# The hand-over between stages of an encoder trunk, put into program order on TensorE, VectorE and ScalarE

## The chip, the cores and the metric

The kernel runs on one core of a Trainium2 chip. A core has TensorE (PE, the matrix products), VectorE (DVE) and GpSimd (POOL) for element-wise work, ScalarE (ACT) for activations and copies, and SyncE (SP), which only starts transfers. Each engine works through its own queue of instructions in order, and waits there on semaphores that other engines raise. The metric is the device time of one execution in microseconds (us).

## The reference

Two layers over 512 tokens of width 1024, in fp32. Each layer is a feed-forward half-step, a mixer with three attentions, and a second feed-forward half-step, each between two RMS norms:

```python
y = swiglu(rmsnorm(h, ffn1_pre_g[l]), ffn1_w_gu[l], ffn1_w_down[l])
h = h + 0.5 * rmsnorm(y, ffn1_post_g[l])
u = rmsnorm(h, mix_pre_g[l]); proj = u @ w_in[l]
...
h = h + rmsnorm(merged @ w_out[l], mix_post_g[l])
y = swiglu(rmsnorm(h, ffn2_pre_g[l]), ffn2_w_gu[l], ffn2_w_down[l])
h = h + 0.5 * rmsnorm(y, ffn2_post_g[l])
```

So a stage ends with a product y, the mean square of y over the width, the new h, and from it the operand of the next stage's first product.

## The kernel before

**Data.** Activations lie transposed: h is eight tiles of 128 features x 512 tokens, and so are y and the operand X. Every fp32 product is made of three matmuls (mm3, L245): high part by high part, high by low, low by high. The high parts are made on ScalarE and the low parts on VectorE: for weights at L201 and L202 (tile w, from the loaded tile wr), for X at L316 and L317 (`operand`: X high = h times the gain, X low = the rest). HALVES are the two halves of 256 tokens.

**The end of a stage** (`end`, L361). All column blocks but the last are made over all 512 tokens. The last block (a feed-forward stage) or the last two (a mixer) are made in two halves by `part` (L390): `part(0)`, then `part(1)`; in a feed-forward stage a half has 22 steps of three matmuls, in a mixer 2 x 8 steps. Each block's y is copied on ScalarE, and its squares are added up in the tile ss (L311). After a part come the *sums*: matmuls of ss with ones (L291), 128x1 each, then a scale by VectorE (L293), a square root on ScalarE (L294) and a reciprocal on VectorE (L295); and the *spread*: matmuls that repeat the resulting scales over 128 partitions (L282), into a PSUM tile at. Then `refresh(i)` (L410) makes the half i of the new h and X: y times the scales for eight tiles on VectorE (L413), h plus y (L416; on VectorE for tiles 2 and 5, on GpSimd for the other six), X high on ScalarE and X low on VectorE.

**The begin of the next stage** (`begin`, L321). The first three column blocks are made in two halves as well, with the weights kept: `dense` over the eight X for the first half (3 blocks x 3 matmuls for each X), `refresh(1)`, then the second half. After that the squares of the new h are added up (L310, L311), and sums and spread over all 512 tokens (`finish_rms`, L338) give rB, by which the stage's products are multiplied. In a feed-forward stage that happens in the middle of the product u1 (L478), in a mixer after the product `second`.

There are five such hand-overs: from a feed-forward stage to a mixer at 344 and 1598 us, from one feed-forward stage to the next at 1238 us, and from a mixer to a feed-forward stage at 884 and 2132 us.

**What sets the order.** The program is written for a tile framework whose scheduler sorts the instructions of every engine by its own model of readiness; the order written in the code is only its input. Inside `tc.manual_schedule(engines=...)` the named engines keep the order of the code instead. The kernel before uses that at none of the places above. Weights are loaded by ScalarE's queue (L188) in tiles of 512 KB, each of which `ensure` (called by `wblk`) turns into two pairs of high and low halves ahead of their use; there are four buffers for these pairs, and some more that are lent for the hand-over.

Of the kernel before, what the change touches and what calls it, by code (L numbers as in the profile page):

```python
# [16 lines left out]
P = 128  # L17
# [94 lines left out]
def encoder_kernel(ctx: ExitStack, tc: tile.TileContext, order, xT, wts, cols, rows, rpb, consts, tables, out):  # L112
# [134 lines left out]
        PE.matmul(acc, w[0], x[1], start=False, stop=False)  # L247
        PE.matmul(acc, w[1], x[0], start=False, stop=stop)  # L248

    def dense(blocks, X, tags=("mm",), cs=WHOLE, accs=None, ws=None, midway=None):  # L250
        accs = accs or [bank(tags[i % len(tags)]) for i in range(len(blocks))]
        n = len(X)
        kept = []
        for k in range(n):
            if midway and k == n // 2:
                midway()
# [7 lines left out]
    def dense1(name, l, c, X, r0=0, tag="mm", midway=None):  # L264
        return dense([(name, l, r0, c)], X, (tag,), midway=midway)[0]

    def split(src, tag="a", scale=None, shape=(P, T)):
        hi = big(tag, F32R, shape, name="hi")
# [16 lines left out]
        return rep[:, : nt * P]  # L285


    def inv_rms(squares, n, nt):
        tot = bank("o")
        for t in range(nt):  # L290
            PE.matmul(tot[:, t : t + 1], squares[:, t * P : (t + 1) * P], ones[:, 0:1], start=True, stop=True)  # L291
# [4 lines left out]
        return spread(r, nt)  # L296

    class Squares:
        def __init__(self):
# [38 lines left out]
    def finish_rms(s, rB):  # L338
        rep = inv_rms(s.acc, D, NT)
        V.tensor_copy(rB, rep)  # L340
        return rep

    def pair(name, dt=F32R):
# [17 lines left out]
    def end(name, l, X, group, tail, gcol, after, hold=()):  # L361

        ys = singles("y")
        y = [ys(b) for b in range(KD)]
        s = Squares()

        def take(b, acc, cs):
            s.add(V if b == KD - 1 else G, acc[:, cs], cs)
            A.activation(y[b][:, cs], acc[:, cs], AF.Copy, scale=gcol(b))

        if hold:
            at = len(order) + (KD - tail) * len(X)
# [11 lines left out]
        def scales(i):  # L384
            hs = HALVES[i]
            return inv_rms(s.acc[:, hs], D, 2)

        held = {}

        def part(i):  # L390
            for m in range(KD - tail, KD):
                acc, cs = bank("mm" if m % 2 else "at"), HALVES[i]
                ks = list(range(len(X)))
                if i and not hold:
                    ks.reverse()
                for n, k in enumerate(ks):
                    if (m, k) not in held:
# [10 lines left out]
        reps, Xn = [], fresh() if after else None  # L408

        def refresh(i):  # L410
            hs = HALVES[i]
            for b in range(KD):
                V.tensor_tensor(out=y[b][:, hs], in0=y[b][:, hs], in1=reps[i], op=ALU.mult)  # L413
            for b in range(KD):
                adder = V if b % 3 == 2 else G
                adder.tensor_tensor(out=h[b][:, hs], in0=h[b][:, hs], in1=y[b][:, hs], op=ALU.add)  # L416
                if after:
                    operand(Xn, i, b, after)
                else:
                    nc.sync.dma_start(out[b * P : (b + 1) * P, hs], h[b][:, hs])  # L420
# [34 lines left out]
    def ffn(l, which, refresh, X):  # L455
# [164 lines left out]
        finish(0, g0, u0)  # L620
        finish(1, g1, u1)
        for m in range(2, PLAIN):
            finish(m, dense1(gu, l, m, X), dense1(gu, l, KF + m, X, tag="at"))
        while later:
            later.pop(0)()
        divide("22")
# [279 lines left out]
    def mixer(l, refresh, X):  # L906
        w = "w_in"
        firsts = [(w, l, 0, QA), (w, l, 0, KA), (w, l, 0, VA)]
        first, s = begin(refresh, X, firsts, [holder("tx")] * 2)
        second = [dense1(w, l, c + 1, X) for c in (QA, KA)[:SECOND]]  # L910
        rB = big("rr", name="rB")
        rep = finish_rms(s, rB)
# [207 lines left out]

    X = fresh()

    def refresh(i):
        for b in range(KD):
            operand(X, i, b, pre(0, 0))

    refresh(0)
    for l in range(L):
        with open_phase("f"):
            refresh, X = ffn(l, 1, refresh, X)  # L1130
# [4 lines left out]
    refresh(1)  # L1135
    assert len(order) == NBLOCKS, (len(order), NBLOCKS)


# [54 lines left out]
```

## Time and profile before

| | |
|---|---|
| median of 3 runs | 2518.18 us (2516.23 to 2518.66) |
| the profiled execution | 2517.49 us, span 2515.7 us |
| mean granted TensorE clock | 0.994 |
| TensorE busy | 2471.4 us (98%) |
| VectorE busy | 1702.3 us (68%) |
| ScalarE busy | 1260.5 us (50%) |
| GpSimd busy | 197.6 us (8%) |

The profile is of one execution. Busy time of an engine is the sum of its instructions' spans; since matmuls are pipelined, one that starts 0.12 us after the one before is shown with a span of 0.28 us, and the pace of TensorE is read from starts. The views used below: the page (a summary), the waits (idle time of an engine put down to the instruction that released it), the windows (busy time and instruction count of each engine in a stretch of time, with the granted clock, 1.00 being full speed), and the timeline (single instructions of an engine with start, duration, line, tiles and, in brackets, the idle time ahead and its releaser; equal neighbours are put together as "x8").

### The profile page before, as it was taken

Reading aid. Unit: us, or ns where it says so; the run is one execution under the profiler, and the core shown is the slowest. Engines: PE = TensorE matmul, PEld = TensorE weight load, DVE = VectorE, ACT = ScalarE, POOL = GpSimd, SP = SyncE. Lnnn points to the kernel's source line nnn. Section 1 sums busy time; section 2 is a strip of 40 time slices with the busy share of each in tenths; the row PEclk is TensorE's granted clock in tenths of the full one; section 3 lists DMA queues with packets and bytes.
Section 4 is the critical chain, followed back from the end, with each engine's and each line's share of the span. In section 5 each row is a group of like instructions: output and inputs, shape, how many; then the busy total and the mean of one; then the engine's idle time right before and its main releaser. Section 6 shows DMA issues by size and latency. Waiting matters only on the chain.

```text
span 2515.7 us, 38188 instructions
## 1 busy us (share of the span) xinstructions
PE 2471.4 (98%) x14586; PEld 2181.1 (87%) x14586; DVE 1702.3 (68%) x3062; ACT 1260.5 (50%) x2447; POOL 197.6 (8%) x177
## 2 busy tenths in 40 slices
PE   9999999999999999999999999999999999999998
PEld 8999888888778889998889998888787788899987
DVE  8877248857767478773388772588676764887723
ACT  6555245645555455553355553546455554555532
POOL 0000020000111120000100000200011112100002
PEclk9999999999999999999999999999999999999999
DMA  4333337434443323333233333374344423233232
GB/s 153 109 106 97 100 101 208 115 109 127 117 126 98 108 65 116 101 101 93 92 93 109 110 93 93 125 197 116 107 126 133 119 90 110 65 116 103 91 103 84
DMA packets 97398, 278.21 MB, mean 111 GB/s; under 512 B 13504, under 2 KB 17984, under 8 KB 97216
## 3 DMA queue, kind: packets, MB, share of 16 engines
q10 hardware_dynamic: 41184, 149.52, 19.5%
q1 hardware_dynamic: 56032, 126.27, 17.7%
q8 instruction: 114, 1.87, 0.3%
q14 instruction: 68, 0.56, 0.1%
HBM read 231.16 MB, written 6.29 MB: 94 GB/s over the span
## 4 chain that ended last, share of the span: by engine, by line
PE 85%; DVE 7%; DMA 4%; issue 1%; SPq 1%; ACT 1%; POOL 1%; POOLq 0%; DVEq 0%; ACTq 0%
PE mm L650 19%; PE mm L248 14%; PE mm L247 14%; PE mm L246 14%; PE at L246 4%; PE at L247 4%; PE at L248 4%; PE at L650 3%; DMA wr<-in_wts_dram 1%; DVE X L317 1%; DMA sh<-raw 1%; PE at L884 1%; DVE y L413 1%; PE at L856 1%; PE o L888 1%
## 5 line engine op out<-in xcount | busy, mean ns | idle before, releaser
L202 DVE TENSOR_TENSOR w<-wr,w 128x512 fp32r<-128x512 f32 x568 | 406.6, 721 | 408.7 <-ACT w L201 406.6
L201 ACT ACTIVATE w<-wr 128x512 fp32r<-128x512 f32 x568 | 354.3, 629 | 554.1 <-PE at L248 269.3
L248 PE MATMUL mm<-X,w 128*128 128x512 f32 (+1 forms) x1096 | 418.5, 383 | 7.2 <-DVE w L202 7.2
L247 PE MATMUL mm<-X,w 128*128 128x512 f32 (+1 forms) x1096 | 419.0, 383 | 4.2 <-DVE X L317 4.2
L246 PE MATMUL mm<-X,w 128*128 128x512 f32 (+1 forms) x1096 | 419.3, 384 | 2.9 <-ACT w L201 1.8
L650 PE MATMUL mm<-lt,h 128*128 128x256 f32 x1024 | 289.8, 283 | 0.0
L650 PE MATMUL mm<-ht,h 128*128 128x256 f32 x1024 | 289.8, 283 | 0.0
L650 PE MATMUL mm<-ht,l 128*128 128x256 f32 x1024 | 289.8, 283 | 0.0
L248 PEld LDWEIGHTS mm<-X,w 128*128 128x128 f32 x1096 | 209.8, 192 | 41.5 <-DVE w L202 8.4
L247 PEld LDWEIGHTS mm<-X,w 128*128 128x128 f32 x1096 | 210.1, 192 | 39.2 <-DVE X L317 6.4
L246 PEld LDWEIGHTS mm<-X,w 128*128 128x128 f32 x1096 | 210.0, 192 | 36.2 <-ACT w L201 2.0
L650 PEld LDWEIGHTS mm<-lt,h 128*128 128x128 f32 x1024 | 196.0, 191 | 0.0
L650 PEld LDWEIGHTS mm<-ht,l 128*128 128x128 f32 x1024 | 196.0, 191 | 0.0
L650 PEld LDWEIGHTS mm<-ht,h 128*128 128x128 f32 x1024 | 196.0, 191 | 0.0
L543 DVE TENSOR_TENSOR r<-wr,wr 128x1024 f32<-128x1024 f32 x64 | 78.5, 1226 | 117.9 <-DMA wr<-in_wts_dram 115.1
L311 POOL TENSOR_TENSOR ss<-ss,sq 128x512 f32<-128x512 f32 (+1 forms) x38 | 47.3, 1245 | 1357.6 <-ACT sq L310 1356.5
L247 PE MATMUL mm<-a,w 128*128 128x512 f32 (+1 forms) x432 | 152.7, 354 | 0.0
L650 PE MATMUL mm<-h,h 128*128 128x256 f32 x512 | 145.7, 285 | 3.4 <-DVE v L704 3.3
L650 PE MATMUL mm<-h,l 128*128 128x256 f32 x512 | 144.9, 283 | 0.0
L650 PE MATMUL mm<-l,h 128*128 128x256 f32 x512 | 144.9, 283 | 0.0
L271 ACT ACTIVATE hi<-at 128x256 fp32r<-128x256 f32 (+2 forms) x168 | 76.5, 473 | 73.1 <-PE at L884 29.4
L247 PE MATMUL mm<-lo,w 128*128 128x512 f32 (+1 forms) x288 | 110.6, 384 | 0.0
(270 smaller groups left out, 5814.7 us busy)
## 6 DMA issues: line engine op xcount, KB each, us to landing
wr<-in_wts_dram ACTq DMA_DIRECT2D x285, 512.0 KB, 3.5
wr<-in_wts_dram SPq DMA_DIRECT2D x130, 512.0 KB, 3.5
st<-hi SPq DMA_DIRECT2D x84, 128.0 KB, 2.4
st<-lo SPq DMA_DIRECT2D x84, 128.0 KB, 3.3
sh<-raw SPq DMA_DIRECT2D x104, 64.0 KB, 3.4
sw<-lo SPq DMA_DIRECT2D x36, 128.0 KB, 3.8
sw<-hi SPq DMA_DIRECT2D x36, 128.0 KB, 2.7
braw<-in_rpb_dram SPq DMA_DIRECT2D x16, 256.0 KB
```

Source lines behind the costliest of these rows:

```text
L201: A.activation(hi, raw, AF.Copy)
L202: V.tensor_tensor(out=lo, in0=raw, in1=f(hi), op=ALU.subtract)
L246: PE.matmul(acc, w[0], x[0], start=start, stop=False)
L247: PE.matmul(acc, w[0], x[1], start=False, stop=False)
L248: PE.matmul(acc, w[1], x[0], start=False, stop=stop)
L271: A.activation(hi, src, AF.Copy)
L311: eng.tensor_tensor(out=self.acc[:, cs], in0=self.acc[:, cs], in1=sq[:, cs], op=ALU.add)
L317: V.scalar_tensor_tensor(out=lo[:, hs], in0=h[b][:, hs], scalar=gcol(b), in1=f(hi)[:, hs], op0=ALU.mult, op1=ALU.subtract)
L413: V.tensor_tensor(out=y[b][:, hs], in0=y[b][:, hs], in1=reps[i], op=ALU.mult)
L543: V.tensor_tensor(out=W[g]["r13"], in0=base, in1=raws[g][0], op=ALU.add)
L650: PE.matmul(acc, ws[i], xs[j], start=start and k == n == 0, stop=stop and k == HK - 1 and n == 2, skip_group_check=True,)
L856: PE.matmul(sp, qs, sk[0][:, j0 * P : j1 * P], start=True, stop=False)
```

## The change

Nothing is computed that was not computed before, with the same instructions on the same engines; what changes is where they stand.

- `inv_rms` is taken apart into `sums` and `spread`, so that the two can be put at different places. `dense` takes a table of hooks: a function to be called ahead of step k.
- TensorE keeps the program's order (`fix`) from `part(0)` on until behind the next stage's `finish_rms` (`loose`).
- In that order the sums of the first half stand ahead of step 4 of `part(1)` (behind 12 matmuls), the spread and `refresh(0)` ahead of step 10 (behind 30). In the next stage's first half, eight steps of nine matmuls, the second half's sums stand ahead of step 2, spread and `refresh(1)` ahead of step 5. The sums for rB stand ahead of step 5 (feed-forward) or 4 (mixer) of the following product, their spread three steps into the third product (feed-forward) or behind the product (mixer).
- In `refresh`, VectorE and ScalarE keep the program's order: first all y and h (y0, h0, y1, h1 and so on, h on the engine it had), then all eight X.

```diff
-        def refresh(i):
-            hs = HALVES[i]
-            for b in range(KD):
-                V.tensor_tensor(out=y[b][:, hs], in0=y[b][:, hs], in1=reps[i], op=ALU.mult)
-            for b in range(KD):
-                adder = V if b % 3 == 2 else G
-                adder.tensor_tensor(out=h[b][:, hs], in0=h[b][:, hs], in1=y[b][:, hs], op=ALU.add)
-                if after:
-                    operand(Xn, i, b, after)
...
+        def refresh(i):
+            hs = HALVES[i]
+            rep = spread(rs[i], 2)
+            with tc.manual_schedule(engines={V.engine, A.engine}):
+                for b in range(KD):
+                    V.tensor_tensor(out=y[b][:, hs], in0=y[b][:, hs], in1=rep, op=ALU.mult)
+                    adder = V if b % 3 == 2 else G
+                    adder.tensor_tensor(out=h[b][:, hs], in0=h[b][:, hs], in1=y[b][:, hs], op=ALU.add)
+                for b in range(KD):
+                    if after:
+                        operand(Xn, i, b, after)
...
-        part(0)
-        reps.append(scales(0))
-        ensure(stream["made"] + (0 if hold else 2))
-        refresh(0)
-        part(1)
-        reps.append(scales(1))
-        return refresh, Xn
+        fix()
+        part(0)
+
+        def first_half():
+            ensure(stream["made"] + (0 if hold else 2))
+            refresh(0)
+
+        part(1, {4: lambda: total(0), 10: first_half})
+        return {2: lambda: total(1), 5: lambda: refresh(1)}, Xn
...
-        accs, ws = dense(first, X, ("mm", "at"), HALVES[0])
-        refresh(1)
+        accs, ws = dense(first, X, ("mm", "at"), HALVES[0], hooks=refresh)
         dense(first, X, (), HALVES[1], accs, ws)
...
-        u1 = dense1(gu, l, KF + 1, X, tag="at", midway=lambda: finish_rms(s, rB))
+        r = []
+        u1 = dense1(gu, l, KF + 1, X, tag="at", hooks={5: lambda: r.append(sums(s.acc, D, NT))})
+        third = dense1(gu, l, 2, X, hooks={3: lambda: finish_rms(r[0], rB)})
+        loose()
```

What this does to the order, at the places that the prediction speaks of:

**VectorE, first hand-over, second half.** The tiles of y are 2756 to 2759 (two tiles in each, hence x2), those of h and X are numbered from h_74 and X_3438 on; L413, L416 and L317 are y, h and X low. Before:

```order
L413 TENSOR_TENSOR y_2756<-y_2756,at_3674 128x256 x2
L413 TENSOR_TENSOR y_2757<-y_2757,at_3674 128x256 x2
L413 TENSOR_TENSOR y_2758<-y_2758,at_3674 128x256 x2
L413 TENSOR_TENSOR y_2759<-y_2759,at_3674 128x256 x2
L317 SCALAR_TENSOR_TENSOR X_3438<-h_74,colt,X_3438 128x256
L317 SCALAR_TENSOR_TENSOR X_3439<-h_75,colt,X_3439 128x256
L416 TENSOR_TENSOR h_76<-h_76,y_2757 128x256
L317 SCALAR_TENSOR_TENSOR X_3441<-h_77,colt,X_3441 128x256
L317 SCALAR_TENSOR_TENSOR X_3442<-h_78,colt,X_3442 128x256
L416 TENSOR_TENSOR h_79<-h_79,y_2758 128x256
```

The same place after (L428 and L430 are y and h there; the L311 between them are the squares of h's first half):

```order
L428 TENSOR_TENSOR y_2756<-y_2756,at_3742 128x256 x2
L428 TENSOR_TENSOR y_2757<-y_2757,at_3742 128x256
L311 TENSOR_TENSOR ss_3879<-ss_3879,sq_3893 128x256
L430 TENSOR_TENSOR h_76<-h_76,y_2757 128x256
L428 TENSOR_TENSOR y_2757<-y_2757,at_3742 128x256
L428 TENSOR_TENSOR y_2758<-y_2758,at_3742 128x256 x2
L311 TENSOR_TENSOR ss_3879<-ss_3879,sq_3896 128x256
L430 TENSOR_TENSOR h_79<-h_79,y_2758 128x256
L428 TENSOR_TENSOR y_2759<-y_2759,at_3742 128x256 x2
L317 SCALAR_TENSOR_TENSOR X_3438<-h_74,colt,X_3438 128x256
L317 SCALAR_TENSOR_TENSOR X_3439<-h_75,colt,X_3439 128x256
```

X_3438, the first X that TensorE needs, stood behind the eight y, and now stands behind the eight y, two h and two additions of squares.

**VectorE, first hand-over, first half**, after the change (L202 makes low parts of weights):

```order
L428 TENSOR_TENSOR y_2757<-y_2757,at_3585 128x256
L428 TENSOR_TENSOR y_2758<-y_2758,at_3585 128x256
L202 TENSOR_TENSOR w_3579<-wr_3577,w_3579 128x512
L202 TENSOR_TENSOR w_3582<-wr_3577,w_3582 128x512
L428 TENSOR_TENSOR y_2758<-y_2758,at_3585 128x256
L430 TENSOR_TENSOR h_79<-h_79,y_2758 128x256
L428 TENSOR_TENSOR y_2759<-y_2759,at_3585 128x256 x2
L317 SCALAR_TENSOR_TENSOR X_3438<-h_74,colt,X_3438 128x256
...
L317 SCALAR_TENSOR_TENSOR X_3445<-h_81,colt,X_3445 128x256
L202 TENSOR_TENSOR w_3628<-wr_3626,w_3628 128x512
L202 TENSOR_TENSOR w_3643<-wr_3626,w_3643 128x512
L311 TENSOR_TENSOR ss_2963<-ss_2963,sq_3667 128x256
```

Two low parts of weights stand among the y, and the addition to ss_2963, which the second half's sums read, stands behind all eight X and two more weights. Before, it stood behind the eight X and three weights, with one weight among the y, one behind the h, and X_3438 and X_3439 ahead of the h.

**TensorE, first hand-over, next stage's first half.** mm and at_3677 are the accumulators of the three blocks, o the sums, at_3742 and at_3674 the spread's result. Before, around the spread:

```order
L246 MATMUL mm_3682<-X_3444,w_3711 128x256
L247 MATMUL mm_3682<-X_3444,w_3711 128x256
L248 MATMUL mm_3682<-X_3444,w_3712 128x256
L246 MATMUL mm_3684<-X_3444,w_3727 128x256
L282 MATMUL at_3674<-cons,rs_3670 128x128 x2
L246 MATMUL at_3683<-X_3438,w_3591 128x256
L247 MATMUL at_3683<-X_3438,w_3591 128x256
```

After:

```order
L248 MATMUL mm_3678<-X_3439,w_3582 128x256
L291 MATMUL o_3697<-ones,ss_2963 128x1 x2
L246 MATMUL mm_3676<-X_3440,w_3582 128x256
...
L248 MATMUL mm_3678<-X_3442,w_3643 128x256
L282 MATMUL at_3742<-cons,rs_3701 128x128 x2
L246 MATMUL mm_3676<-X_3443,w_3643 128x256
```

Before, two of the three blocks ran over the X first, the sums stood at the fifth X, and behind the spread the whole third block (24 matmuls) was left beside the rest of the two. After, all three blocks take each X together, the sums stand behind two X (18 matmuls), and behind the spread three X (27 matmuls) are left.

More of the change, by code (lines that the diff above doesn't have):

```diff
@@ L254, in dense @@
         for k in range(n):
-            if midway and k == n // 2:
-                midway()
+            if k in hooks:
+                hooks[k]()
             x = X[k][0][:, cs], X[k][1][:, cs]
@@ L285, in spread, with sums @@
         return rep[:, : nt * P]
-    def inv_rms(squares, n, nt):
+    def sums(squares, n, nt):
         tot = bank("o")
@@ L295, in inv_rms @@
         V.reciprocal(out=r[:, :nt], in_=r[:, :nt])
-        return spread(r, nt)
+        return r
     class Squares:
@@ L336, in begin, with finish_rms, fix, loose @@
         return accs, s
-    def finish_rms(s, rB):
-        rep = inv_rms(s.acc, D, NT)
+    def finish_rms(r, rB):
+        rep = spread(r, NT)
         V.tensor_copy(rB, rep)
         return rep
+    fixed = []
+    def fix():
+        fixed.append(tc.manual_schedule(engines={PE.engine}))
+        fixed[-1].__enter__()
+    def loose():
+        if fixed:
+            fixed.pop().__exit__(None, None, None)
     def pair(name, dt=F32R):
@@ L382, in end, with part @@
                 take(m + b, acc, WHOLE)
-        def scales(i):
-            hs = HALVES[i]
-            return inv_rms(s.acc[:, hs], D, 2)
         held = {}
-        def part(i):
+        def part(i, hooks={}):
+            step = 0
             for m in range(KD - tail, KD):
@@ L396, in part @@
                 for n, k in enumerate(ks):
+                    if step in hooks:
+                        hooks[step]()
+                    step += 1
                     if (m, k) not in held:
@@ L407, in end, with total @@
         A.activation(dummy, y[KD - tail - 1][:, 0:1], AF.Sqrt, scale=0.0)
-        reps, Xn = [], fresh() if after else None
+        rs, Xn = [], fresh() if after else None
+        def total(i):
+            rs.append(sums(s.acc[:, HALVES[i]], D, 2))
         def refresh(i):
             hs = HALVES[i]
-            for b in range(KD):
-                V.tensor_tensor(out=y[b][:, hs], in0=y[b][:, hs], in1=reps[i], op=ALU.mult)
-            for b in range(KD):
-                adder = V if b % 3 == 2 else G
-                adder.tensor_tensor(out=h[b][:, hs], in0=h[b][:, hs], in1=y[b][:, hs], op=ALU.add)
-                if after:
-                    operand(Xn, i, b, after)
-                else:
-                    nc.sync.dma_start(out[b * P : (b + 1) * P, hs], h[b][:, hs])
-        part(0)
-        reps.append(scales(0))
-        ensure(stream["made"] + (0 if hold else 2))
-        refresh(0)
-        part(1)
-        reps.append(scales(1))
-        return refresh, Xn
+            rep = spread(rs[i], 2)
[7 more added lines that the diff above has]
+                        operand(Xn, i, b, after)
+                    else:
+                        nc.sync.dma_start(out[b * P : (b + 1) * P, hs], h[b][:, hs])
+        fix()
+        part(0)
+        def first_half():
[3 more added lines that the diff above has]
+        return {2: lambda: total(1), 5: lambda: refresh(1)}, Xn
     def align():
@@ L622, in ffn @@
         for m in range(2, PLAIN):
-            finish(m, dense1(gu, l, m, X), dense1(gu, l, KF + m, X, tag="at"))
+            finish(m, third if m == 2 else dense1(gu, l, m, X), dense1(gu, l, KF + m, X, tag="at"))
         while later:
@@ L909, in mixer @@
         first, s = begin(refresh, X, firsts, [holder("tx")] * 2)
-        second = [dense1(w, l, c + 1, X) for c in (QA, KA)[:SECOND]]
         rB = big("rr", name="rB")
-        rep = finish_rms(s, rB)
+        r = []
+        second = [dense1(w, l, c + 1, X, hooks={4: lambda: r.append(sums(s.acc, D, NT))}) for c in (QA, KA)[:SECOND]]
+        rep = finish_rms(r[0], rB)
+        loose()
         rB8 = big("rr", name="rB8")
@@ L1121, in encoder_kernel, with put @@
     X = fresh()
-    def refresh(i):
+    def put(i):
         for b in range(KD):
             operand(X, i, b, pre(0, 0))
-    refresh(0)
+    put(0)
+    refresh = {KD - 1: lambda: put(1)}
     for l in range(L):
@@ L1134, in encoder_kernel @@
             refresh, X = ffn(l, 2, refresh, X)
-    refresh(1)
+    for at in sorted(refresh):
+        refresh[at]()
+    loose()
     assert len(order) == NBLOCKS, (len(order), NBLOCKS)
```

6 lines of the change are left out of this document (3 added, 3 removed).

## The prediction

> **What bounds the kernel now.** I read the page first, then the windows of the five hand-overs, then what TensorE waits for there, and last the single instructions.
>
> ```profile
> PE 2471.4 (98%) x14586; PEld 2181.1 (87%) x14586; DVE 1702.3 (68%) x3062; ACT 1260.5 (50%) x2447; POOL 197.6 (8%) x177
> PE 85%; DVE 7%; DMA 4%; issue 1%; SPq 1%; ACT 1%; POOL 1%; POOLq 0%; DVEq 0%; ACTq 0%
> ```
>
> TensorE is busy 98% of the span and carries 85% of the chain that ended last; VectorE carries 7%. As the change takes no matmul away, it can only gain or lose what TensorE idles, or runs at a lower clock, at the hand-overs. Their size: each window below goes from the first half-width product of `part(0)` to the first full-width product of the next stage.
>
> ```profile
> 344.20:388.72 44.52, 40.51 (x294) 39.41 (x292) 32.40 (x74) 24.65 (x56) 10.76 (x13) 0.88 0.46 152
> 884.26:919.78 35.52, 33.25 (x257) 32.40 (x256) 26.67 (x60) 23.19 (x56) 14.24 (x17) 0.95 0.12 37
> 1238.10:1278.66 40.56, 37.65 (x294) 36.57 (x293) 30.12 (x69) 24.49 (x56) 10.78 (x13) 0.96 0.25 77
> 1597.84:1638.19 40.35, 36.33 (x293) 35.23 (x292) 31.49 (x73) 24.57 (x56) 10.76 (x13) 1.00 0.49 160
> 2132.13:2167.89 35.76, 33.48 (x257) 32.42 (x256) 26.69 (x60) 23.20 (x56) 14.26 (x17) 0.95 0.12 38
> ```
>
> The columns are the elapsed time, then busy time and count of PE, weight loads, DVE, ACT and POOL, then the granted clock. What would the work take without a wait? Rows of TensorE at the second hand-over (mixer to feed-forward):
>
> ```profile
> 892.05 0.50 PE L291 MATMUL o<-ones,ss 128*128 128x1 f32 x4
> 892.42 0.36 PE L248 MATMUL mm<-hi,w 128*128 128x256 f32 x1
> 893.24 0.71 PE L282 MATMUL at<-cons,rs 128*128 128x128 f32 x4
> 893.71 0.36 PE L246 MATMUL at<-hi,w 128*128 128x256 f32 x1
> 893.91 0.28 PE L247 MATMUL at<-lo,w 128*128 128x256 f32 x1
> 894.03 0.28 PE L248 MATMUL at<-hi,w 128*128 128x256 f32 x1
> 897.66 0.39 PE L247 MATMUL mm<-X,w 128*128 128x256 f32 x1 [0.48 <-DVE X L317]
> 897.88 0.28 PE L248 MATMUL mm<-X,w 128*128 128x256 f32 x1
> 900.69 0.70 PE L291 MATMUL o<-ones,ss 128*128 128x1 f32 x4 [1.30 <-DVE ss L311]
> 902.04 0.41 PE L248 MATMUL mm<-X,w 128*128 128x256 f32 x1
> 902.25 0.41 PE L247 MATMUL mm<-X,w 128*128 128x256 f32 x1
> ```
>
> From start to start, a half-width matmul takes 894.03 - 893.91 = 0.12 us, the sums 0.37, the spread 0.47; in a stretch at half clock a matmul takes 902.25 - 902.04 = 0.21. A feed-forward stage's hand-over is 2 x 22 x 3 matmuls of `part` and 2 x 8 x 9 of the next stage, 276, plus two sums and two spreads (1.7): 276 x 0.12 + 1.7 = 34.8 us. A mixer's is 2 x 48 + 144 = 240: 30.5 us. The excess over that is 9.7, 5.0, 5.8, 5.55 and 5.3 us, in all **31.3 us**, and this is all that the change can win.
>
> Part of it is the clock:
>
> ```profile
> 361.71:365.12 3.41, 1.68 (x12) 1.28 (x11) 3.41 (x10) 3.27 (x8) 0.00 (x0) 1.00 0.65 220
> 368.53:371.94 3.41, 3.41 (x18) 3.41 (x18) 2.16 (x7) 1.12 (x4) 0.00 (x0) 0.50 0.20 32
> 897.60:901.01 3.41, 2.04 (x13) 1.66 (x14) 3.41 (x6) 2.79 (x9) 2.33 (x3) 1.00 0.00 0
> 1617.81:1621.22 3.41, 1.88 (x16) 1.80 (x15) 3.41 (x8) 3.41 (x10) 0.00 (x0) 1.00 0.22 80
> 2150.29:2153.71 3.42, 3.42 (x19) 3.42 (x18) 2.61 (x8) 2.66 (x10) 0.00 (x0) 0.50 0.00 0
> ```
>
> The clock falls to 0.50 in stretches of 3.41 us (the second and last row; there are six such at the hand-overs, two running at the first). A stretch costs 3.41 x (1 - 0.12/0.213) = 1.49 us, six 8.9. The stretch ahead of a fall shows only 12 or 13 matmuls (first and third row: counted by starts, TensorE worked 0.34 of it); one with 16 (fourth row) was followed by full clock. So on this trace some 2.05 us without starts in one stretch halves the next, and 1.9 don't. That leaves 31.3 - 8.9 = **22.4 us** of waits.
>
> [...]
>
> **The change part by part.** The scales' way (sums, root, spread) and the work are the same; what counts is when the first X of a half is ready, and how much TensorE has left by then. The rows of VectorE and GpSimd, second half of the first hand-over, then first half:
>
> ```profile
> 372.94 2.73 DVE L413 TENSOR_TENSOR y<-y,at 128x256 f32<-128x256 f32 x8 [1.16 <-PE at L282]
> 375.59 1.84 DVE L317 SCALAR_TENSOR_TENSOR X<-h,colt,X 128x256 fp32r<-128x256 f32 x2
> 377.36 0.95 DVE L416 TENSOR_TENSOR h<-h,y 128x256 f32<-128x256 f32 x1
> 379.03 0.42 DVE L416 TENSOR_TENSOR h<-h,y 128x256 f32<-128x256 f32 x1
> 380.16 0.42 DVE L311 TENSOR_TENSOR ss<-ss,sq 128x256 f32<-128x256 f32 x1
> 373.44 4.60 POOL L416 TENSOR_TENSOR h<-h,y 128x256 f32<-128x256 f32 x6 [12.24 <-DVE y L413]
> 356.33 4.87 POOL L416 TENSOR_TENSOR h<-h,y 128x256 f32<-128x256 f32 x6 [9.42 <-DVE y L413]
> 372.29 0.60 PE L282 MATMUL at<-cons,rs 128*128 128x128 f32 x4
> 357.24 1.07 DVE L202 TENSOR_TENSOR w<-wr,w 128x512 fp32r<-128x512 f32 x1
> 362.07 0.68 DVE L202 TENSOR_TENSOR w<-wr,w 128x512 fp32r<-128x512 f32 x1
> 362.68 2.45 DVE L317 SCALAR_TENSOR_TENSOR X<-h,colt,X 128x256 fp32r<-128x256 f32 x6
> 893.99 2.74 DVE L413 TENSOR_TENSOR y<-y,at 128x256 f32<-128x256 f32 x8 [0.80 <-PE at L282]
> ```
>
> An X low takes 2.45/6 = 0.41 with GpSimd idle (362.68; it is idle from 361.20 to 373.44) and 0.88 to the next start (377.36 - 375.59, for two) while GpSimd runs its six h (373.44 to 378.04). An h lasts 0.42 alone against 0.95 beside GpSimd, a weight's low part 0.68 against 1.07; as neighbours overlap by some 0.08, I count 0.33 and 0.88, 0.6 and 1.0. A y, which reads PSUM, is 2.73/8 = 0.34 beside GpSimd as well. From the spread's start to the first y: 372.94 - 372.29 = 0.65 and 893.99 - 893.24 = 0.75; I take 0.70.
>
> [...]
>
> *First X of a half.* Before, it follows the eight y: 2.73 + 0.88 = 3.6 us after the first y starts. After:
> - mixer, both halves, and the feed-forward stages' second half where the next is a mixer: eight y (2.7), two h (1.76), two ss (0.33 to 0.88 each, the first beside GpSimd: 1.0), X low 0.41: 5.85. In the second halves the X high and the ss wait a little on ScalarE's squares: 6.35. The third hand-over has no ss in its second half: 5.35.
> - a feed-forward stage's first half has two weights of 1.0 in place of the ss, part of the last GpSimd adds run beside the X: 6.8.
>
> *Cover, and stall A (end of `part(1)`).* Feed-forward: the spread stands behind 30 of 66 matmuls, so 36 x 0.12 + 0.47 = 4.8 us are left; X is ready at 0.70 + 6.8 = 7.5: **2.65 us** of waiting. Mixer: 18 matmuls are left, 2.63 us, X at 0.70 + 5.85 = 6.55: **3.9**, where before the row at 897.66 waits 0.48.
>
> *Stall B (second half's sums, feed-forward).* They stand behind two X, 18 x 0.12 = 2.2 us after the first X. What they read, the last ss, stands behind X1 to X7 and two weights: 3.15 + 2 x 0.6 + 0.35 = 4.7 us after the first X. **2.55 us.** In a mixer that ss comes before the X: nothing; the 1.30 at 900.69 goes.
>
> *Stall C (end of the next stage's first half).* Behind the spread 27 matmuls: 27 x 0.12 + 0.47 = 3.7 us. X at 0.70 + 6.35 = 7.05: **3.3 us**, 2.35 at the third hand-over. Before, a whole block was put off behind the spread, and the waits there were small:
>
> ```profile
> 379.34 0.39 PE L246 MATMUL mm<-X,w 128*128 128x256 f32 x1 [0.45 <-ACT X L316]
> 381.02 0.38 PE L247 MATMUL mm<-X,w 128*128 128x256 f32 x1 [1.07 <-DVE X L317]
> PE mm L248 <- DVE w L202: 7.2, 6, 1.5
> ```
>
> Once the first X is there, the others follow every 0.41 us, and TensorE needs 9 x 0.12 = 1.08 for each: the later X no longer stall. Nor do the weights: the 7.2 us of the last row go, since both weights are made ahead of the X; that gain is inside the 22.4.
>
> *Sum of the waits.* Feed-forward to mixer, twice: 2.65 + 2.55 + 3.3 = 8.5. Feed-forward to feed-forward: 7.55. Mixers, twice: 3.9 + 3.3 = 7.2. In all 39.0; the matmul behind a wait is followed after 0.22 instead of 0.12 us (897.66 to 897.88), for 13 waits 1.3: **40.3 us**, against 22.4: +17.9.
>
> *Clock.* Stretches fall without regard to the kernel, so a wait of I us leaves 2.05 empty in one of them with a chance of (I - 0.69)/3.41: 0.94 and 0.77 for a mixer's A and C, 0.55 and 0.77 (once 0.49) for a feed-forward stage's B and C. Behind a feed-forward stage's A the slower products would only eat into the wait B, so it isn't counted. That makes 2 x 1.71 + 2 x 1.32 + 1.04 = 7.1 halved stretches, at 1.4 us (a little of each lies on waits) 10 us, against 8.9: **+1.1**.
>
> *Costed at nothing.* rB in the feed-forward stages comes some 3 us later (12 full-width matmuls, each twice a half-width one's 0.12), covered by the rest of the third product, 15 such matmuls, some 3.5 us; without that cover at most 1 us for each of four. A mixer's sums for rB, a step later or earlier in a product of 24. The out transfers at the very end (the same six GpSimd adds stand ahead) and the bias transfers moved on SP's queue: -1 to +1 us.
>
> Sum: 17.9 + 1.1 = +19.0 us on the profiled execution, 2517.5, which lies 0.7 under the median shown: 2536.5. The two unknowns (how GpSimd's adds and VectorE interleave, how the stretches fall) lean towards less, as a wait that halves the clock also slows the work that covers the next one; I take **2536 us**.
>
> **The rivals.** A measurement of this kernel can tell about 0.2%, 5 us, from no change.
>
> 1. *VectorE is not held up in the new order; faster.* With h in a row behind each y, GpSimd and VectorE could fall into step, and h, ss and weights cost 0.33, 0.33 and 0.6. The first X then comes at 2.7 + 0.66 + 0.66 + 0.41 = 4.4 (with weights 4.9). A: feed-forward 0.8, mixer 2.5; C: 1.4; B stays. Waits: 3 x 4.7 + 2 x 3.9 = 22, clock 3: 25 against 31.3, 2511 us; with the ss behind the X as well, 2508. It decides where the h costs under 0.5 us. Against it: both X low beside GpSimd in the rows above are slow, and the h at 377.36 is 0.95.
> [...]
> 3. *The clock stays down from wait to wait*: 12 stretches, 18 us: 2543 to 2546. At the first hand-over two ran on end.
> 4. *It comes out even*: X highs or weights come early enough for A and B to halve, 19 us down to 5 or less: 2513 to 2522.
>
> **How the numbers follow.** Forecast, with its own range of 2526 to 2543: 0.50; rival 2, inside that range: 0.14; rival 3: 0.08; these are all slower: 0.72. Even: 0.14. Faster (rival 1): 0.14. Below 2515 lie rival 1 and a little of the even case, above 2545 a part of rival 3: the range is 2515 to 2545.
>
> **What would show it.** In the changed profile's waits, TensorE's first matmul of each half of the next stage would wait 2.3 to 3.9 us on X, and the sums of the three feed-forward hand-overs 2.5 us on ss; 5 windows 3 to 4 us longer each; X low behind all y at 5.3 to 6.8 us after the first y. I am wrong if X comes within 4.5 us of the first y, or if TensorE's waits on X stay under 1 us.

## The result and the profile after

| | before | after |
|---|---|---|
| median | 2517.81 us (4 runs) | 2539.69 us (4 runs, 2538.94 to 2542.05) |
| ratio | | 1.0089, 95% interval 1.0072 to 1.0107 |
| profiled execution | 2517.49 us, span 2515.7 us | 2539.74 us, span 2537.9 us |
| TensorE busy | 2471.4 us | 2473.5 us |

The changed kernel is 22 us slower; 2536 was forecast, in a range of 2515 to 2545. The same five windows of the changed kernel, cut from the first half-width product of `part(0)` to the first full-width product of the next stage:

```profile
344.56:390.26 45.70, 39.40 (x293) 38.72 (x292) 33.90 (x76) 24.68 (x56) 11.21 (x13) 0.89 0.47 155
889.64:929.98 40.34, 34.02 (x257) 33.60 (x256) 28.13 (x63) 23.21 (x56) 14.37 (x17) 0.92 0.13 44
1249.63:1293.31 43.68, 37.08 (x294) 36.50 (x292) 32.41 (x71) 24.52 (x56) 11.16 (x13) 0.96 0.26 85
1611.30:1658.99 47.69, 39.67 (x293) 39.08 (x292) 34.60 (x77) 24.81 (x56) 11.20 (x13) 0.89 0.47 150
2150.26:2191.84 41.58, 35.26 (x257) 34.85 (x256) 28.17 (x63) 23.21 (x56) 14.37 (x17) 0.88 0.14 42
```

They are 1.2, 4.8, 3.1, 7.3 and 5.8 us longer than before, 22.3 in all, and the span grew by 22.2: the whole loss lies in the hand-overs. They grew so unevenly because the stretches of 3.41 us at half clock went from 3, 1, 1, 0 and 1 to 3, 2, 1, 3 and 3 (a clock of 0.89 over 45.70 us is three of them). (Between them single stretches moved, the first mixer's inside by +3.8 and the second's by -2.7, and cancel out.) What TensorE waits for, in the view of waits:

```profile
PE mm L247 <- DVE X L317: 27.5, 10, 3.5
PE o L291 <- DVE ss L311: 7.4, 4, 2.6
```

Before, X cost TensorE 4.2 us and ss 3.7, in the same view; the 7.2 us on weights (L202) are gone, as forecast:

```profile
PE mm L247 <- DVE X L317: 4.2, 7, 1.1
PE o L291 <- DVE ss L311: 3.7, 3, 1.3
```

Ten waits on X are two for each of five hand-overs: stalls A and C. The sums' row has the three stalls B, and one wait at the end of the program. One each of A, B and C in the timeline of TensorE:

```profile
905.77 0.38 PE L247 MATMUL mm<-X,w 128*128 128x256 f32 x1 [3.46 <-DVE X L317]
1269.19 0.39 PE L247 MATMUL mm<-X,w 128*128 128x256 f32 x1 [2.58 <-DVE X L317]
1274.07 0.47 PE L291 MATMUL o<-ones,ss 128*128 128x1 f32 x3 [2.59 <-DVE ss L311]
381.65 0.39 PE L247 MATMUL mm<-X,w 128*128 128x256 f32 x1 [2.85 <-DVE X L317]
```

The first is A of a mixer's end, the second and third A and B of a feed-forward stage's, the last C. Why X is late is read from VectorE, here in the first half of the third hand-over, and then some rows of the second hand-over's first half (a mixer's end):

```profile
1262.33 1.08 DVE L428 TENSOR_TENSOR y<-y,at 128x256 f32<-128x256 f32 x3
1263.44 0.42 DVE L430 TENSOR_TENSOR h<-h,y 128x256 f32<-128x256 f32 x1
1263.79 0.74 DVE L428 TENSOR_TENSOR y<-y,at 128x256 f32<-128x256 f32 x2
1264.45 2.42 DVE L202 TENSOR_TENSOR w<-wr,w 128x512 fp32r<-128x512 f32 x2
1266.79 0.41 DVE L428 TENSOR_TENSOR y<-y,at 128x256 f32<-128x256 f32 x1
1267.23 0.43 DVE L430 TENSOR_TENSOR h<-h,y 128x256 f32<-128x256 f32 x1
1267.57 0.74 DVE L428 TENSOR_TENSOR y<-y,at 128x256 f32<-128x256 f32 x2
1268.23 4.16 DVE L317 SCALAR_TENSOR_TENSOR X<-h,colt,X 128x256 fp32r<-128x256 f32 x8
1272.31 1.28 DVE L202 TENSOR_TENSOR w<-wr,w 128x512 fp32r<-128x512 f32 x2
1273.52 0.41 DVE L311 TENSOR_TENSOR ss<-ss,sq 128x256 f32<-128x256 f32 x1
```

```profile
900.08 1.08 DVE L428 TENSOR_TENSOR y<-y,at 128x256 f32<-128x256 f32 x3 [2.10 <-PE at L282]
903.53 0.43 DVE L311 TENSOR_TENSOR ss<-ss,sq 128x256 f32<-128x256 f32 x1 [0.92 <-ACT sq L310]
904.87 4.09 DVE L317 SCALAR_TENSOR_TENSOR X<-h,colt,X 128x256 fp32r<-128x256 f32 x8
```

The first X starts 1268.23 - 1262.33 = 5.9 us after the first y, and 4.8 in the mixer's end. The eight X of these rows take some 0.5 us each, but the first two are slower, with GpSimd's last two h beside them (1.60 us from 1268.13 and from 904.71 on). The first X alone, of both places and of the third hand-over's second half, whose first y starts at 1279.95:

```profile
1268.23 0.91 DVE L317 SCALAR_TENSOR_TENSOR X<-h,colt,X 128x256 fp32r<-128x256 f32 x1
904.87 0.84 DVE L317 SCALAR_TENSOR_TENSOR X<-h,colt,X 128x256 fp32r<-128x256 f32 x1
1283.66 0.97 DVE L317 SCALAR_TENSOR_TENSOR X<-h,colt,X 128x256 fp32r<-128x256 f32 x1
```

So the first X is ready 6.8 and 5.6 us after the first y, against 6.8 and 5.85 forecast, and 4.7 in the last of the three places. In the other four second halves it is ready after 6.1 us (0.83 us from 380.77 on, with the first y at 375.49). Two rows are worth a second look: the two weights among the y take 2.42 us, and the ss at 1273.52, which the sums at 1274.07 wait for, stands behind eight X and two more weights.

### The profile page after: what moved, and what is told of

The parts are those of the page before. It is cut to its first block, busy times and chain, and to the rows that moved or that the text cites. A ratio compares the mean times of both kernels' runs of the same rounds, so it can differ in the third digit from the quotient of the medians.

```text
span 2537.9 us, 38154 instructions
## 1 busy us (share of the span) xinstructions
PE 2473.5 (97%) x14586; PEld 2186.9 (86%) x14586; DVE 1704.8 (67%) x3062; ACT 1259.3 (50%) x2447; POOL 198.1 (8%) x177
## 4 chain that ended last, share of the span: by engine, by line
PE 82%; DVE 9%; DMA 4%; issue 2%; ACT 2%; POOL 1%; SPq 1%; POOLq 0%; DVEq 0%; ACTq 0%
PE mm L670 19%; PE mm L247 13%; PE mm L248 13%; PE mm L246 13%; PE at L246 4%; PE at L248 4%; PE at L247 4%; PE at L670 3%; DMA wr<-in_wts_dram 2%; DVE w L202 1%; PE at L904 1%; DMA sh<-raw 1%; DVE y L428 1%; DVE X L317 1%; PE o L908 1%
## 5 line engine op out<-in xcount | busy, mean ns | idle before, releaser
L202 DVE TENSOR_TENSOR w<-wr,w 128x512 fp32r<-128x512 f32 x568 | 409.2, 725 | 433.8 <-ACT w L201 432.0
L247 PE MATMUL mm<-X,w 128*128 128x512 f32 (+1 forms) x1096 | 420.3, 384 | 27.5 <-DVE X L317 27.5
L311 POOL TENSOR_TENSOR ss<-ss,sq 128x512 f32<-128x512 f32 (+1 forms) x38 | 46.9, 1235 | 1368.2 <-ACT sq L310 1367.1
```

What stands on the lines that cost most here:

```text
L202: V.tensor_tensor(out=lo, in0=raw, in1=f(hi), op=ALU.subtract)
L311: eng.tensor_tensor(out=self.acc[:, cs], in0=self.acc[:, cs], in1=sq[:, cs], op=ALU.add)
```

## The experiments

Each ratio is to the kernel before in the same round of measurements, whose median there was 2519.9 to 2520.7 us.

**VectorE's and ScalarE's order alone.** TensorE is left to the scheduler:

```diff
 def fix():
-    fixed.append(tc.manual_schedule(engines={PE.engine}))
-    fixed[-1].__enter__()
+    return
```

> The new order of VectorE and ScalarE alone: TensorE is left to the scheduler again, with the hooks standing as they do after the change. Theory 1 (the time is lost because the first X of a half comes behind all y and the h, 5.3 to 6.4 us after the first y): the first product of each half still waits on X for 1.5 to 3.5 us, and the time is 2528 to 2542 us. Rival (TensorE's fixed order is what costs): 2515 to 2523 us.

Measured: 2536.87 us median, ratio 1.0069 (1.0044 to 1.0094). Its waits:

```profile
PE mm L247 <- DVE X L317: 24.7, 10, 3.7
PE o L291 <- DVE ss L311: 4.5, 3, 1.6
```

Again ten waits on X. Those at the feed-forward stages' ends are nearly as long as in the changed kernel (2.3 us), those at the mixers' ends are 1.1, with 1.6 us on the sums ahead of them. With TensorE free, the scheduler puts the feed-forward stages' sums later and their B is gone, but the spread comes later too, and C grows there (3.3 to 3.7 us, against 1.4 to 2.9). Theory 1 holds, but for the 1.1 us at the mixers' ends, where at least 1.5 was expected: this half alone costs most of what the change costs.

**TensorE's order alone.** VectorE and ScalarE are left to the scheduler, and refresh is written as before:

```diff
-            with tc.manual_schedule(engines={V.engine, A.engine}):
+            if hs:
                 for b in range(KD):
                     V.tensor_tensor(out=y[b][:, hs], in0=y[b][:, hs], in1=rep, op=ALU.mult)
+                for b in range(KD):
                     adder = V if b % 3 == 2 else G
                     adder.tensor_tensor(out=h[b][:, hs], in0=h[b][:, hs], in1=y[b][:, hs], op=ALU.add)
-                for b in range(KD):
                     if after:
                         operand(Xn, i, b, after)
```

> TensorE's new order alone: VectorE and ScalarE are left to the scheduler, with refresh written as in the kernel before. Theory 1: the first X comes 3.6 us after the first y instead of 5.7 to 6.3, so the waits at the mixers' ends fall from 3.5 to about 1.5 us, those ahead of each second half from 2.9 to under 1 us; the feed-forward stages' sums wait longer, 3 to 5 us, since they are reached earlier and their ss does not come earlier. Sum 2522 to 2533 us. Rival (TensorE's fixed order is what costs): 2535 to 2540 us.

Measured: 2522.16 us, ratio 1.0011 (0.9997 to 1.0024): no change that can be told from none, and just at the lower end of the forecast. The waits, and A of a mixer and B of a feed-forward stage:

```profile
PE o L291 <- DVE ss L311: 11.5, 6, 3.3
PE mm L247 <- DVE X L317: 11.0, 13, 1.6
```

```profile
900.14 0.39 PE L247 MATMUL mm<-X,w 128*128 128x256 f32 x1 [1.42 <-DVE X L317]
1263.98 0.35 PE L291 MATMUL o<-ones,ss 128*128 128x1 f32 x2 [3.25 <-DVE ss L311]
```

With X ahead of the h again, a mixer's A falls from 3.46 to 1.42 us, and X costs 11.0 us instead of 27.5. B is 3.25 instead of 2.6 us: what A gives, B takes in part, since its ss comes no earlier. So the two halves of the change are not alike: VectorE's and ScalarE's order costs 0.7 to 0.8%, TensorE's about nothing by itself (it takes the waits on weights away and adds those on ss).

**The clock.** In the changed kernel TensorE has longer waits, and the clock halves more often. Windows of the changed kernel: a stretch ahead of a fall and the halved one behind it, twice; then one that is not followed by a fall (PE's count is the first in parentheses, the clock the third column from the end):

```profile
902.77:906.18 3.41, 0.41 (x3) 0.41 (x4) 2.65 (x6) 3.20 (x8) 2.30 (x4) 1.00 0.00 0
906.18:909.60 3.42, 3.42 (x19) 3.42 (x17) 2.78 (x7) 2.56 (x7) 0.12 (x1) 0.50 0.00 0
1643.46:1646.87 3.41, 1.48 (x13) 1.28 (x11) 3.41 (x8) 2.21 (x5) 2.02 (x4) 1.00 0.81 308
1646.87:1650.29 3.42, 2.49 (x11) 2.50 (x12) 3.42 (x8) 2.55 (x8) 1.46 (x2) 0.50 0.81 307
377.11:380.52 3.41, 1.69 (x15) 1.49 (x13) 3.41 (x8) 2.17 (x6) 2.10 (x3) 1.00 0.79 300
```

Three or thirteen matmuls in a stretch: halved next. Fifteen: not. These counts include matmuls that began ahead of the stretch; by their starts in the timeline the thirteen are 11 and the fifteen 12, so that 2.1 us without starts were followed by a fall and 2.0 were not. This agrees with the border that the prediction read from the trace of before (2.05 and 1.9), but it is no sharper than that: a stretch with 12 starts was followed by a fall in the kernel before (first row), and with VectorE's and ScalarE's order alone, a stretch with thirteen counted, TensorE waiting in its first 1.8 us, was so as well (second row):

```profile
378.77:382.18 3.41, 1.90 (x14) 1.57 (x13) 3.41 (x10) 2.35 (x7) 0.00 (x0) 1.00 0.73 206
376.23:379.64 3.41, 1.59 (x13) 1.59 (x14) 3.41 (x8) 2.74 (x7) 1.67 (x3) 1.00 0.91 345
```

There are twelve halved stretches in the changed kernel's hand-overs, against six before and 7.1 forecast. To price them, matmuls of constants into an unused bank were put into the waits:

```diff
+        def fill(n):
+            o = bank("o")
+            for _ in range(n):
+                PE.matmul(o[:, :P], ones, ident, start=True, stop=True)
...
+        fill(gap[0])
         accs, ws = dense(first, X, ("mm", "at"), HALVES[0], hooks=refresh)
+        fill(gap[0] and 12)
```

(and `fill(12)` ahead of a feed-forward stage's second sums)

> The changed kernel, with 12 matmuls (20 at a mixer's end) of constants put into each of the 13 waits of TensorE; they write a bank that nothing reads and fit into the waits. Theory 1: the eleven halved stretches of the clock at the hand-overs cost 16 us of the 53.6 us of excess, nearly all beside the waits; without them the time is 2523 to 2529 us, and the waits on X stay where they end now. Rival (the slow stretches lie under the waits and cost little): 2536 to 2541 us.

Measured: 2536.22 us, ratio 1.0066 (1.0043 to 1.0089). That is in the rival's range, and no stretch in the hand-overs is halved any more, but the run doesn't answer the question: each of these matmuls shows as two of 0.11 us, so that the groups were about as long as the waits of a feed-forward stage, and about a us longer than a mixer's A. The five windows are 209.7 us together, 9.3 less than in the changed kernel; the second mixer's inside, which wasn't edited, is 5.1 us longer (496.4 against 491.3). The row for twelve of them:

```profile
361.33 2.84 PE L350 MATMUL o<-cons,ones 128*128 128x128 f32 x24
```

So once more with 9, 13, 9 and 6 in place of 12, 20, 12 and 12:

> As the run before with filled waits, but with so few matmuls of constants that each group (which showed two passes of 0.11 us for every matmul there) ends inside its wait: 9 ahead of a feed-forward hand-over's first X and 13 ahead of a mixer's, 9 ahead of the sums, 6 ahead of the second half. Theory 1: the clock stays at 1.00 through all hand-overs, the waits end where they end in the changed kernel, and the twelve halved stretches (3.41 us each, 17.9 us in all) are won but for 1.7 us at the first hand-over, where a slow stretch lay under a wait: 14 to 17 us under the changed kernel, that is 0.2 to 0.4% above the kernel before. Rival (the clock costs little): less than 5 us won, 0.7 to 0.9% above the kernel before.

Measured: 2532.16 us, ratio 1.0042 (1.0029 to 1.0056). Its first and last hand-over, where the clock is 1.00 (and 0.96, with one stretch left):

```profile
344.54:388.14 43.60, 40.95 (x342) 40.39 (x340) 34.50 (x77) 24.67 (x56) 11.20 (x13) 1.00 0.53 169
2139.38:2178.90 39.52, 36.76 (x295) 36.35 (x294) 27.97 (x63) 23.09 (x56) 14.36 (x17) 0.96 0.15 47
```

All five together are 207.2 us, against 219.0 in the changed kernel: without eleven of the twelve halved stretches the hand-overs are **11.8 us** shorter. The ratios say the same, 0.0047 of 2518 us, with intervals that lie apart. That is less than the 14 to 17 forecast: eleven stretches of 1.49 would be 16.4, but some of each lies on a wait, and waits grew once the products ahead of them ran at full clock: with the filling counted in, B at the first hand-over from 0.9 to 2.6 us, and C at the mixers' two from 2.9 to 3.5. The rival, under 5 us, is out.

**The first X early, TensorE's order kept.** If the late X is the cause, an order of VectorE's with an early X must win most of the loss back:

```diff
-                    adder = V if b % 3 == 2 else G
+                    adder = V if after or b % 3 == 2 else G
                     adder.tensor_tensor(out=h[b][:, hs], in0=h[b][:, hs], in1=y[b][:, hs], op=ALU.add)
+                    if after and b:
+                        operand(Xn, i, b - 1, after)
+                if after:
+                    operand(Xn, i, KD - 1, after)
                 for b in range(KD):
-                    if after:
-                        operand(Xn, i, b, after)
-                    else:
+                    if not after:
                         nc.sync.dma_start(out[b * P : (b + 1) * P, hs], h[b][:, hs])
```

> The changed kernel with another order in refresh: all h but the last stage's on VectorE, and X low of a tile directly behind the next tile's h, so that the first X comes 2 to 3 us after the first y and GpSimd runs beside no X. TensorE's order stays. Theory 1: the waits at the end of a stage's last product and ahead of the second half fall under 0.6 us, the feed-forward stages' sums wait some 1.7 us, and each later X some 0.25 us; 2505 to 2516 us. Rival (TensorE's fixed order is what costs): above 2525 us.

Measured: 2516.99 us, ratio 0.9986 (0.9974 to 0.9998), a us above what theory 1 expected.

```profile
PE o L291 <- DVE ss L311: 8.5, 4, 2.4
PE mm L247 <- DVE X L317: 2.7, 8, 0.5
```

The waits on X are 2.7 us in all, none over 0.5, with TensorE's order unchanged; the rival is out. The hand-overs take 191.2 us, 27.8 less than in the changed kernel and 5.5 less than before. The 5.5 us don't reach the time, for the first mixer's inside, from the first hand-over's end to the next one's start, is 6.0 us longer than before (495.54 us there, one execution each):

```profile
386.34:887.91 501.57, 491.64 (x2366) 402.93 (x2365) 347.64 (x765) 261.03 (x557) 49.66 (x34) 0.99 0.44 122
```

It was run a second time, unchanged:

> The order tile by tile once more, on another chip or another hour, as its first interval only just left out no change. Theory 1: 0.05 to 0.25% under the kernel before; rival (the first time was chance): 0.0 to 0.1% above it.

Measured: 2519.59 us, ratio 0.9994 (0.9980 to 1.0008): 0.06% under, at the edge of what theory 1 expected, with an interval that holds no change. Its profile shows how much one execution differs from another: hand-overs of 195.1 us with four halved stretches instead of one, and 497.3 us for the first mixer's inside. So this version undoes the loss, and that it beats the kernel before is not shown.

**Beside GpSimd.** The same order with h back on GpSimd for six tiles:

```diff
-                    adder = V if after or b % 3 == 2 else G
+                    adder = V if b % 3 == 2 else G
```

> The order tile by tile, but with h on GpSimd for six of eight tiles, as in the changed kernel. Theory 1 (GpSimd's h slow VectorE's X low and h to 0.9 us each): nothing is won by the six h that VectorE is spared, X low is seen at 0.8 to 1.0 us beside GpSimd, and the time is 0 to 8 us above that of the order with h on VectorE. Rival (no such slow-down): VectorE's tile takes 0.75 us instead of 1.07, and the time is 3 to 8 us less.

Measured: 2522.45 us, ratio 0.9996 (0.9984 to 1.0008), 0.1% above the first run of the order with h on VectorE. This kernel differs from the changed one in nothing but the place of the X among the h, and the loss is gone: the late X is the cause. X low of both, grouped:

```profile
L317 DVE SCALAR_TENSOR_TENSOR X<-h,colt,X 128x256 fp32r<-128x256 f32 x96 | 53.7, 567 | 6.2 <-ACT X L316 5.5
```

```profile
L317 DVE SCALAR_TENSOR_TENSOR X<-h,colt,X 128x256 fp32r<-128x256 f32 x96 | 45.2, 480 | 1.2 <-ACT X L316 1.2
```

Beside GpSimd's h (first row) the mean is 567 ns and some take 0.94 us; without them (second) it is 480. VectorE is spared 60 h and gains nothing, so the 3 to 8 us of the rival are out; how much of that is the longer X and how much that an h on GpSimd takes 0.93 us on average at this run's first hand-over (twelve of them, 11.2 us), instead of 0.42, on the way to its X, this run doesn't tell.

**The rest of B.** Three attempts on the 2.4 us that the sums still wait, all on the order tile by tile.

```diff
-s.add(V if b == KD - 1 else G, acc[:, cs], cs)
+s.add(V if b == KD - 1 and cs != HALVES[1] else G, acc[:, cs], cs)
...
-return {2: lambda: total(1), 5: lambda: refresh(1)}, Xn
+return {3: lambda: total(1), 5: lambda: refresh(1)}, Xn
```

> The order tile by tile, with two more edits against the one wait that it left, 2.4 us ahead of the second half's sums in three hand-overs: those sums one step later (step 3), and the last block's second addition to ss on GpSimd, which is idle there. Theory 1: that wait falls to 0.2 to 1.2 us in each of the three, 4 to 6 us in all: 0.3 to 0.5% under the kernel before. Rival (VectorE is full there and only moves the wait to X): less than 2 us won.

Measured: 2523.13 us, ratio 1.0003 (0.9986 to 1.0020). At the hand-overs the theory holds (their sum is 190.2 us, the sums wait 0.3 us, no stretch is halved), but the time is no better. The first mixer's inside, from the first hand-over's end to the next one's start, before and here:

```profile
388.72:884.26 495.54, 489.38 (x2367) 401.57 (x2365) 344.40 (x759) 261.14 (x557) 49.67 (x34) 1.00 0.44 123
```

```profile
383.75:893.19 509.44, 495.36 (x2366) 405.09 (x2365) 345.56 (x767) 261.52 (x557) 49.42 (x34) 0.99 0.45 120
```

13.9 us are lost there, and 5.7 in the second mixer, where nothing was edited. Not all of it is these edits' doing: the order tile by tile, without them, had 501.6 and 492.5 us there, and the profiled execution was the slowest of its ten (2530.57 us). Next, the squares of the new h behind the second half, by a region of fixed order that lasts from `refresh(1)` to the squares:

> As the run with later sums, and the squares of the new h stand behind the whole second half on VectorE and ScalarE, so that a tile takes VectorE 0.34 + 0.33 + 0.39 = 1.07 us instead of 1.40, against TensorE's 1.08. Theory 1: each of the five second halves is up to 2 us shorter where the scheduler puts no other work between, the squares stay covered by the next product: 4 to 8 us less than the run with later sums. Rival (the squares, now later, hold up rB and the products behind it): the same or more.

Measured: 2539.97 us, ratio 1.0074 (1.0045 to 1.0102). The hand-overs are down to 188.3 us, but the sums for rB now wait (L291 waits 10.4 us on ss in all), and the mixers' insides are as long as in the run before. Both mechanisms of the expectation were there, and the rival's is the larger. Last, the later step alone:

> The order tile by tile (h on VectorE, GpSimd idle there), with the second half's sums one step later, ahead of step 3, and nothing else. Theory 1: the 2.4 us that the sums waited for ss in three hand-overs become 1.3, as TensorE does the third X in the meantime (9 x 0.12 us); the mixers' inner order stays as in the order tile by tile, so nothing is lost there: 0 to 3 us under the order tile by tile, 0.1 to 0.3% under the kernel before. Rival (the root and the reciprocal behind the sums are late as well, and the spread takes the wait over): the same as the order tile by tile.

Measured: 2518.85 us, ratio 0.9988 (0.9975 to 1.0000): as the order tile by tile. The rival is right: the sums wait 1.2 instead of 2.4 us, but the spread waits 2.1. VectorE at that place:

```profile
370.25 0.16 DVE L293 TENSOR_SCALAR ms<-o 128x2 f32<-128x2 f32 x1
371.65 0.88 DVE L317 SCALAR_TENSOR_TENSOR X<-h,colt,X 128x256 fp32r<-128x256 f32 x2
372.44 0.16 DVE L295 RECIPROCAL rs<-rs 128x2 f32<-128x2 f32 x1
```

The reciprocal, 0.16 us long, stands behind two X and others, 2.2 us behind the scale that it belongs to. The mixers' insides are 501.7 and 492.2 us here, as in the order tile by tile (501.6 and 492.5), while the two runs with the addition on GpSimd have 509.4 and 499.6, then 507.5 and 499.3. So it is that addition that goes with some 6 to 8 us more in each. These are single executions, and the order tile by tile alone differed by 4 us from one to the other. How an addition at the hand-over costs time inside a mixer was not tried apart: that the scheduler sorts the mixer anew is a guess.

## Why the prediction was right

The time came out 3.7 us above the forecast, by the mechanism forecast: X comes late, and TensorE waits for it. That the sum is so near is in part luck, as two of its terms are wrong in opposite ways. Point by point:

- **The first X.** Right: ready 4.7 to 6.8 us after the first y, against 5.35 to 6.8, and X is what TensorE waits for in all ten places. The 4.7, at the third hand-over's second half, is close to the 4.5 that would have spoken against the forecast. (The 5.3 to 6.4 us in an expectation above took the first X at the mean of its eight, 0.5 us.) Undoing only the place of X (the order tile by tile, with h on either engine) undoes the loss. That X was ready after 3.6 us before holds for seven of ten halves; in the feed-forward stages' first halves, where a weight stood among the y, it was 4.8.
- **Stall A.** 2.58 (2.65 forecast) for feed-forward stages, 3.46 (3.9) for mixers. This is luck in part, as errors cancel: each h cost 0.42, not 0.88 (at the first hand-over it was GpSimd's h beside one of them that was long, 0.95 us from 358.45 on), but the weights took 1.2, not 1.0, and the first X itself 0.84 to 0.91, not 0.41. At the mixers' ends VectorE also stood still for 0.92 us ahead of ss (the row at 903.53).
- **Stall B.** 2.59 at the third and fourth hand-over (2.55 forecast), 0.89 at the first, where halved products ahead of it (0.21 us from start to start) filled the time.
- **Stall C.** 2.85 to 2.87 (3.3 forecast), 1.43 at the third hand-over (2.35). The extra 0.5 us for ScalarE's squares in second halves was not there: VectorE does not stand still ahead of X, which is ready after 6.1 us, not 6.35. At the third hand-over the two h took 0.42 and 0.55, not 0.88 each.
- **The sum of the waits** was sized too high: the 13 waits are 33.6 us, 35.7 with the 0.16 by which a matmul's shown span hides the start of each, against 39.0. Of these 3.3 us less, B at the first hand-over makes 1.5, the five C 1.9 and the mixers' A 0.6; the other A and B are 0.7 above the forecast.
- **The clock** was sized too low. The falls, eight, are near the 7.1 forecast, but the prediction counted one halved stretch for each. At the first, fourth and fifth hand-over two or three ran on end: the halved stretch at 1646.87 above has eleven matmuls, and the next one, to 1653.70, is halved too. That makes twelve, as in rival 3. Of the excess of 53.6 us (219.0 less the 165.4 that the prediction counts for the work), the waits and the slower matmuls behind them (35.7 and 1.3) leave 16.6 us for the clock, against 10 forecast; filling the waits won 11.8 of them, as waits grew in exchange.
- **The windows** were to be 3 to 4 us longer each. Only the third is (3.1); that was wrong, with the sum right.
- **Rivals.** Rival 1 had its condition half fulfilled (an h of 0.42 in the first halves), but the first X didn't come at 4.4 to 4.9: the weights took twice as long, and X itself was slow. Rival 2, inside the forecast's range of times, is out: each of the eight falls came behind a stretch with matmuls in it, 3 to 13 by the windows' count. Rival 3 had the count of stretches right, but took each at its full price; the time stayed under its 2543 us.
- **Costed at nothing**: right in sum, -0.1 us outside the hand-overs.

## What to carry to other kernels

When an order is written by hand, ask first which single instruction the waiting engine needs next, and count what stands ahead of it on each queue: here two h, and in most places one or two other steps, ahead of the first X put it 1.0 to 2.5 us later (3.6 to 4.8 us after the first y, then 4.7 to 6.8) at each of ten places, though not one instruction was added. Look, too, at the other waits that the same busy engine feeds: here, with the first X earlier, the sums waited 3.25 us instead of 2.6 (TensorE's order alone), and with the sums a step later, 1.2 instead of 2.4, the spread waited 2.1. And with an automatic scheduler, look at the stages that were not edited as well: with one addition moved at the hand-over, the mixers' insides were 6 to 8 us longer.

## What the runs showed of the hardware

- Beside GpSimd it is not always VectorE's instruction that is long. In the first half of the first hand-over an h on VectorE takes 0.42 us, and GpSimd's h that starts 0.08 us behind it takes 0.95 (its first, at 357.76, took 0.75). In the second half GpSimd's h starts first: it is done at 377.61, and VectorE's, begun at 376.94, takes 0.96 and is done 0.29 us behind it. (GpSimd's takes 0.92 itself; it began while an ss of VectorE's ran, which was done at 377.02.) The rows:

```profile
358.37 0.42 DVE L430 TENSOR_TENSOR h<-h,y 128x256 f32<-128x256 f32 x1
358.45 0.95 POOL L430 TENSOR_TENSOR h<-h,y 128x256 f32<-128x256 f32 x1
376.69 0.92 POOL L430 TENSOR_TENSOR h<-h,y 128x256 f32<-128x256 f32 x1
376.94 0.96 DVE L430 TENSOR_TENSOR h<-h,y 128x256 f32<-128x256 f32 x1
```

  In both pairs the one that starts later is long (0.95 and 0.96 us), and ends last.
- A weight's low part of 128x512 among GpSimd's h took 1.2 us (2.42 for two), against 0.64 alone (1.28 for two at 1272.31).
- In each of the two profiles the falls of the clock at the hand-overs stand a whole number of 3.413 us apart: in the kernel before they are at 365.12, 382.18, 901.01, 1259.41 and 2150.29, or 0, 5, 157, 262 and 523 times 3.413 us behind the first; in the changed kernel the first three are at 363.46, 906.18 and 919.83, or 0, 159 and 163 times. That agrees with the prediction's "without regard to the kernel".
- A stretch of 3.41 us with 11 starts of half-width matmuls was followed by half the clock, one with 12 wasn't; in other runs of this case the border is as near as that, but not always on the same side. Filling waits with matmuls that nothing needs won 11.8 us, though some waits grew.
